# Gathers of the expert groups written in eight pieces and the sums to the tokens in two, between the phases of the chunks

## The chip, the cores and the metric

The kernel runs on one core of one Trainium2 chip. The metric is device time in microseconds, the median of several executions. The engines are TensorE (PE, its weight loads listed apart as PEld), VectorE (DVE), ScalarE (ACT), GpSimd (POOL) and SyncE (SP), which issues nearly all loads from HBM here.

## What is computed

A two-layer decoder trunk on 256 tokens and 16 meta tokens, width 1024. Layer 0 ends in a dense SwiGLU, layer 1 in a mixture of eight experts, of which each token takes two. The change touches only that mixture:

```python
def moe_swiglu(h, router_w, w_gate, w_up, w_down):
    logits = jnp.einsum('btd,de->bte', h, router_w).astype(jnp.float32)
    top_logits, top_idx = lax.top_k(logits, TOP_K)
    top_w = jax.nn.softmax(top_logits, axis=-1)
    combine = jnp.sum(jax.nn.one_hot(top_idx, N_EXPERTS, dtype=jnp.float32) * top_w[..., None], axis=-2)
    out = jnp.zeros_like(h)
    for e in range(N_EXPERTS):
        out = out + combine[..., e:e + 1] * swiglu(h, w_gate[e], w_up[e], w_down[e])
    return out
```

An expert's three matrices are 1024x3584, 1024x3584 and 3584x1024 in float32.

## The kernel before

Everything ahead of the experts (attention, short convolution, the gated recurrence, the dense layer, the router) is the same in both kernels.

**Experts and their order.** The router ranks the experts by their number of tokens. Rank 0 to 3 are Wide (L1085): up to 128 tokens, held as a high and a low half of 128 columns each. Rank 4 to 7 are Narrow (L1112): up to 64 tokens, high and low half side by side in 128 columns. Experts are put in groups that share one gathered matrix of tokens: group 0 is Wide 0 alone, groups 1 to 3 are a Narrow and then a Wide expert (4 and 1, 5 and 2, 6 and 3), group 4 is Narrow 7 alone. So the order is Wide 0, Narrow 4, Wide 1, Narrow 5, Wide 2, Narrow 6, Wide 3, Narrow 7 (L1189). `experts` (L1146) runs over them, and within an expert over seven chunks of 512 hidden columns (c = 0 to 6). A second call stands in a branch for experts with more tokens than fit (L1192) and is not taken with these inputs.

**A chunk.** `gate_up` (L1030) forms the gate products (tile psg), calls `between`, and forms the up products (psu). `between` (L1175) holds, once for a group, `weights` (the tokens' weights, tile wsp), and always `turn` of the chunk before: PE transposes the hidden values (hps), ACT and DVE split them. After `gate_up`, `finish` (L1160) forms the down products of the chunk before (tile y). A Wide chunk has 24 gate, 24 up and 24 down matmuls of 512 columns, a Narrow one 16 of each.

**Weights.** `MoveWeights` (L840) loads 1 MB at a time into one of seven buffers (six loads to a chunk), and each half is split in two: ACT copies the high part (h_g, h_u, h_d, L856) and DVE subtracts for the low part (l_g, l_u, l_d, L857). Seven pairs of such halves can be ahead.

**The gather.** `Group.__init__` (L994) multiplies the normed tokens (hnh, hnl) by a one-hot matrix (oh). For each of eight 128-row pieces k there are four matmuls (tile gat), one ACT copy and one DVE cast into x (L999 to L1006). It runs whole, ahead of chunk 3 of the last expert of the group before (L1171). The tile gat comes from `wtile` (L834), a pool of two PSUM banks that the weights' tile wsp, the turn of the one-hot matrix (cps) and the sums (sc) share.

**The sums.** When an expert's last down products are done, `combine` (L1068) goes over two halves of 512 columns: ACT and DVE make the weighted result (yh, yl; one buffer each), four matmuls spread it to the tokens (sc, L1079 and L1080), and two DVE adds (L1081) put it on the residual hst. As the down products run one chunk late, this stands after the up products of chunk 0 of the next expert.

**Order on the engines.** The source gives an order of priority. The build then puts each engine's instructions in a fixed order, in which an instruction whose inputs are ready can stand ahead of some that the source names first; each engine works through that order.

Of the kernel before, what the change touches and what calls it, by code (L numbers as in the profile page):

```python
# [19 lines left out]
P = 128  # L20
D = 1024
KD = D // P
# [29 lines left out]
def trunk(ctx: ExitStack, tc: tile.TileContext, x, meta, n1g, n2g, w_in, qng, kng, dlam,  # L52
# [937 lines left out]
    class Group:  # L990
# [3 lines left out]
        def __init__(self, wq_, nq_, oh):  # L994
            self.oh, self.w, self.n = oh, wq_, nq_
            self.x = mo.tile([P, KD, 3 * P], F32R, tag="x", bufs=2, name="x")
            h0, h1 = 0 if wq_ is not None else P, P if nq_ is None else P + 64
            l0, l1 = 2 * P if nq_ is None else P + 64, 3 * P if wq_ is not None else 2 * P
            for k in range(KD):  # L999
                ps = wtile("gat")  # L1000
                for src, o, a0, a1 in ((hnh, 0, h0, h1), (hnl, 256, l0, l1)):
                    for t in range(2):
                        PE.matmul(ps[:, o:o + a1 - a0], src[:, t, k * P:(k + 1) * P], oh[:, t, a0:a1],
                                  start=(t == 0), stop=(t == 1))
                A.activation(self.x[:, k, h0:h1], ps[:, 0:h1 - h0], AF.Copy)
                V.tensor_copy(self.x[:, k, l0:l1], ps[:, 256:256 + l1 - l0])  # L1006
# [13 lines left out]
    class Expert:  # L1020
# [47 lines left out]
        def combine(self, ct):  # L1068

            ws = self.g.ws[:, self.i, 0:1]  # L1070
            for n in range(2):
                ns = slice(n * 512, n * 512 + 512)
# [3 lines left out]
                V.scalar_tensor_tensor(yl, self.y[n], ws, yh.bitcast(F32), op0=ALU.mult, op1=ALU.subtract)  # L1076
                for t in range(2):
# [4 lines left out]
                    if self.last:  # L1082
                        nc.sync.dma_start(out[0, t * P:(t + 1) * P, ns], hst[:, t, ns])

# [61 lines left out]
    def experts(plan, first=None):  # L1146

        def group(pl):
            w = next((q for q, k in pl if k is Wide), None)
            n = next((q for q, k in pl if k is Narrow), None)  # L1150
            oh = oh0 if first and pl is plan[0] else one_hot(w, n, pos_s, sel_s)
            return Group(w, n, oh)

        flat = [(gi, q, k) for gi, pl in enumerate(plan) for q, k in pl]
        groups = {0: group(plan[0])}
        if first:
            new_phase("silu_and_others")
        prev = None

        def finish(x, c, ht):  # L1160
# [3 lines left out]
            if c == NCE - 1:  # L1164
                x.combine(ct)

        for n, (gi, q, kind) in enumerate(flat):
            x = kind(place[q], groups[gi])
            x.last = n == len(flat) - 1
            for c in range(NCE):  # L1170
                if c == 3 and n + 1 < len(flat) and flat[n + 1][0] != gi:  # L1171
                    groups[gi + 1] = group(plan[gi + 1])
                ht = []

                def between():  # L1175
                    if c == 0 and not hasattr(groups[gi], "ws"):
                        groups[gi].weights()
                    if prev is not None:
                        ht.append(prev[0].turn(prev[2]))
                if first and n == 0 and c == 1:  # L1180
                    residual(1)
                h = x.gate_up(c, between)
                if prev is not None:
                    finish(prev[0], prev[1], ht[0])
                prev = (x, c, h)
        finish(prev[0], prev[1], prev[0].turn(prev[2]))

    residual(0)
    experts([[(0, Wide)]] + [[(q + WIDE - 1, Narrow), (q, Wide)] for q in range(1, WIDE)] + [[(NE - 1, Narrow)]], True)  # L1189

    cnt = nc.values_load(cmaxi[0:1, 0:1], min_val=0, max_val=S + P // 2)
    with tc.If(cnt > P):  # L1192
        V.tensor_single_scalar(pos_s[:, :, 0:WIDE], pos_s[:, :, 0:WIDE], -float(P), op=ALU.add)
        V.tensor_single_scalar(pos_s[:, :, WIDE:], pos_s[:, :, WIDE:], -float(P // 2), op=ALU.add)
        experts([[(q, Wide)] for q in range(NE)])
# [30 lines left out]
```

## Time and profile before

| | us |
|---|---|
| median of three executions | 1830.02 |
| their range | 1829.35 to 1831.63 |
| the profiled execution | 1831.06 |
| its span, first to last instruction | 1829.3 |

In the profile each engine has its busy time; "idle before" is the time an engine stood still ahead of an instruction, with what ended it (the releaser). TensorE's granted clock is given as a share of 2.4 GHz, so 0.50 is 1.2 GHz. The stretches below are cut from the end of a chunk's last gate matmul to the end of the next chunk's last one, so a stretch holds one chunk's worth of up, down and gate products.

### The profile page before, as it was taken

Reading aid. Unit: us, or ns where it says so; the run is one execution under the profiler, and the core shown is the slowest. Engines: PE = TensorE matmul, PEld = TensorE weight load, DVE = VectorE, ACT = ScalarE, POOL = GpSimd, SP = SyncE. Lnnn points to the kernel's source line nnn. Section 1 sums busy time; section 2 is a strip of 40 time slices with the busy share of each in tenths; the row PEclk is TensorE's granted clock in tenths of the full one; section 3 lists DMA queues with packets and bytes.
Section 4 is the critical chain, followed back from the end, with each engine's and each line's share of the span. In section 5 each row is a group of like instructions: output and inputs, shape, how many; then the busy total and the mean of one; then the engine's idle time right before and its main releaser. Section 6 shows DMA issues by size and latency. Waiting matters only on the chain.

```text
span 1829.3 us, 27972 instructions
## 1 busy us (share of the span) xinstructions
PE 1763.9 (96%) x10613; PEld 1515.4 (83%) x10613; DVE 1468.0 (80%) x1934; ACT 1179.2 (64%) x1587; POOL 110.4 (6%) x137
## 2 busy tenths in 40 slices
PE   8999999999999999999999999999999999999997
PEld 7888999999999889998788767776677866787665
DVE  7667757877567577577889999989998899988997
ACT  4366444544443664446778887768877688877786
POOL 5201201100011003012000000000000000000000
PEclk9999999999999999998999999999999999999999
DMA  7333554555554236656989999999999899999996
GB/s 214 101 99 93 169 177 162 165 181 185 167 179 139 70 95 189 187 196 234 343 321 368 366 394 371 360 330 352 394 387 372 315 345 395 394 351 352 362 388 232
DMA packets 266123, 479.96 MB, mean 262 GB/s; under 512 B 7636, under 2 KB 115228, under 8 KB 265980
## 3 DMA queue, kind: packets, MB, share of 16 engines
q1 hardware_dynamic: 265472, 477.20, 73.8%
q8 instruction: 85, 1.39, 0.3%
q0 software_dynamic: 368, 0.86, 0.2%
q14 instruction: 58, 0.48, 0.1%
q10 hardware_dynamic: 140, 0.04, 0.0%
HBM read 477.01 MB, written 1.05 MB: 261 GB/s over the span
## 4 chain that ended last, share of the span: by engine, by line
PE 49%; DVE 11%; issue 3%; ACT 3%; POOL 0%; DVEq 0%; ACTq 0%; POOLq 0%
DVE l_g L857 5%; PE psu L1119 4%; PE psu L1118 3%; PE y L1091 3%; PE y L1090 3%; PE y L1092 3%; PE psu L1091 3%; PE psg L1091 3%; PE psu L1092 3%; PE psu L1090 3%; PE psg L1092 2%; PE psg L1090 2%; PE proj L230 2%; PE proj L229 2%; PE proj L228 2%
## 5 line engine op out<-in xcount | busy, mean ns | idle before, releaser
L230 PE MATMUL proj<-hgh,lo_in 128*128 128x272 f32 (+1 forms) x1024 | 297.2, 290 | 4.6 <-DVE lo_in L224 4.6
L228 PE MATMUL proj<-hgh,hi_in 128*128 128x272 f32 (+1 forms) x1024 | 297.8, 291 | 0.2 <-DVE z L357 0.2
L229 PE MATMUL proj<-hgl,hi_in 128*128 128x272 f32 (+1 forms) x1024 | 296.9, 290 | 0.0
L857 DVE TENSOR_TENSOR l_u<-r_u,h_u 128x1024 fp32r<-128x1024 f32 x224 | 265.3, 1220 | 28.2 <-ACT h_u L856 25.1
L857 DVE TENSOR_TENSOR l_d<-r_d,h_d 128x1024 fp32r<-128x1024 f32 x224 | 264.8, 1220 | 17.4 <-ACT h_d L856 15.4
L857 DVE TENSOR_TENSOR l_g<-r_g,h_g 128x1024 fp32r<-128x1024 f32 x224 | 265.4, 1220 | 5.8 <-ACT h_g L856 5.4
L223 ACT ACTIVATE hi_in<-raw_in 128x1024 fp32r<-128x1024 f32 x128 | 135.0, 1058 | 165.6 <-PE proj L229 150.3
L856 ACT ACTIVATE h_u<-r_u 128x1024 fp32r<-128x1024 f32 x224 | 227.4, 1053 | 15.6 <-PE y L1092 9.0
L856 ACT ACTIVATE h_g<-r_g 128x1024 fp32r<-128x1024 f32 x224 | 226.5, 1053 | 11.9 <-PE psu L1092 5.4
L856 ACT ACTIVATE h_d<-r_d 128x1024 fp32r<-128x1024 f32 x224 | 223.2, 1052 | 7.1 <-PE psg L1092 5.9
L230 PEld LDWEIGHTS proj<-hgh,lo_in 128*128 128x128 f32 x1024 | 193.9, 189 | 6.6 <-DVE lo_in L224 5.5
L228 PEld LDWEIGHTS proj<-hgh,hi_in 128*128 128x128 f32 x1024 | 194.1, 190 | 2.8 <-issue 1.1
L229 PEld LDWEIGHTS proj<-hgl,hi_in 128*128 128x128 f32 x1024 | 193.6, 189 | 2.4 <-issue 1.3
L224 DVE TENSOR_TENSOR lo_in<-raw_in,hi_in 128x1024 fp32r<-128x1024 f32 x128 | 158.5, 1240 | 33.6 <-ACT hi_in L223 33.3
L1119 PE MATMUL psg<-l_g,x 128*128 128x512 f32 x224 | 98.7, 441 | 20.3 <-DVE l_g L857 20.0
L1119 PE MATMUL psu<-l_u,x 128*128 128x512 f32 x224 | 98.2, 438 | 1.5 <-DVE l_u L857 1.5
L1119 PEld LDWEIGHTS psg<-l_g,x 128*128 128x128 f32 x224 | 41.9, 187 | 63.3 <-DVE l_g L857 57.6
L1091 PE MATMUL psg<-l_g,x 128*128 128x512 f32 x224 | 91.2, 407 | 3.1 <-DVE l_g L857 2.8
L1090 PE MATMUL psg<-h_g,x 128*128 128x512 f32 x224 | 90.3, 403 | 0.0
L1118 PE MATMUL psu<-h_u,x 128*128 128x512 f32 x224 | 90.1, 402 | 0.0
L1090 PE MATMUL psu<-h_u,x 128*128 128x512 f32 x224 | 89.9, 401 | 0.0
L1092 PE MATMUL psg<-h_g,x 128*128 128x512 f32 x224 | 89.8, 401 | 0.0
(404 smaller groups left out, 4124.5 us busy)
## 6 DMA issues: line engine op xcount, KB each, us to landing
r_g<-in_moe_w_gate_dram SPq DMA_DIRECT2D x112, 1024.0 KB, 7.0
r_u<-in_moe_w_up_dram SPq DMA_DIRECT2D x112, 1024.0 KB, 7.7
r_d<-in_moe_w_down_dram SPq DMA_DIRECT2D x110, 1024.0 KB, 7.9
raw_in<-in_w_in_dram SPq DMA_DIRECT2D x64, 1024.0 KB, 5.9
raw_br<-in_w_branch_dram SPq DMA_DIRECT2D x12, 1024.0 KB, 5.5
raw_fg<-in_ffn_w_gate_dram SPq DMA_DIRECT2D x11, 1024.0 KB, 5.3
raw_fu<-in_ffn_w_up_dram SPq DMA_DIRECT2D x11, 1024.0 KB
raw_wo<-in_w_out_dram SPq DMA_DIRECT2D x8, 1024.0 KB, 4.9
```

The costliest lines, as they stand in the source:

```text
L223: A.activation(hi, r, AF.Copy)
L224: V.tensor_tensor(lo, r, hi.bitcast(F32), op=ALU.subtract)
L228: PE.matmul(ps, sh, mh, start=first, stop=False)
L229: PE.matmul(ps, sh, ml, start=False, stop=False)
L230: PE.matmul(ps, sl, mh, start=False, stop=last)
L856: ih = raw_ins(A.activation(hi, r, AF.Copy))
L857: il = raw_ins(V.tensor_tensor(lo, r, hi.bitcast(F32), op=ALU.subtract))
L1090: PE.matmul(ps, st[0], hi, start=first, stop=False)
L1091: PE.matmul(ps, st[0], lo, start=False, stop=False)
L1092: PE.matmul(ps, st[1], hi, start=False, stop=last)
L1118: PE.matmul(ps, st[0], hi, start=first, stop=False)
L1119: PE.matmul(ps, st[0], lo, start=False, stop=last)
```

## The change

The experts keep their order. Three things move.

1. A group is made without its gather; `gather(k)` does one piece. Making the group and its one-hot matrix stands at the start of the chunk three ahead of the group's first one (two ahead for group 1). The eight pieces go on a list, `todo`.
2. `short` takes pieces off the list: two while more than four are left, else one, after the gate products (in `between`, ahead of `turn`) and after the up products, and one after the down products. What is left is done when the group begins. Group 0's gather is written whole at the start, as before.
3. `combine` makes the first half of the weighted result at once and returns two steps: the first puts half 0 to the tokens and makes half 1, the second puts half 1. They go to the head of the list; the first is taken right away by the `short()` behind `finish`, the second by the one after the next chunk's gate products.

The calls are turned from a plan of experts into a flat list of chunks, with the same chunks in the same order.

```diff
--- before.py
+++ after.py
@@ -996,14 +996,17 @@
             self.x = mo.tile([P, KD, 3 * P], F32R, tag="x", bufs=2, name="x")
             h0, h1 = 0 if wq_ is not None else P, P if nq_ is None else P + 64
             l0, l1 = 2 * P if nq_ is None else P + 64, 3 * P if wq_ is not None else 2 * P
-            for k in range(KD):
-                ps = wtile("gat")
-                for src, o, a0, a1 in ((hnh, 0, h0, h1), (hnl, 256, l0, l1)):
-                    for t in range(2):
-                        PE.matmul(ps[:, o:o + a1 - a0], src[:, t, k * P:(k + 1) * P], oh[:, t, a0:a1],
-                                  start=(t == 0), stop=(t == 1))
-                A.activation(self.x[:, k, h0:h1], ps[:, 0:h1 - h0], AF.Copy)
-                V.tensor_copy(self.x[:, k, l0:l1], ps[:, 256:256 + l1 - l0])
+            self.h, self.l = (h0, h1), (l0, l1)
+
+        def gather(self, k):
+            (h0, h1), (l0, l1) = self.h, self.l
+            ps = wtile("gat")
+            for src, o, a0, a1 in ((hnh, 0, h0, h1), (hnl, 256, l0, l1)):
+                for t in range(2):
+                    PE.matmul(ps[:, o:o + a1 - a0], src[:, t, k * P:(k + 1) * P], self.oh[:, t, a0:a1],
+                              start=(t == 0), stop=(t == 1))
+            A.activation(self.x[:, k, h0:h1], ps[:, 0:h1 - h0], AF.Copy)
+            V.tensor_copy(self.x[:, k, l0:l1], ps[:, 256:256 + l1 - l0])
 
         def weights(self):
 
@@ -1067,13 +1070,18 @@
 
         def combine(self, ct):
 
+
             ws = self.g.ws[:, self.i, 0:1]
-            for n in range(2):
-                ns = slice(n * 512, n * 512 + 512)
+
+            def prepare(n):
                 yh = mo.tile([P, 512], F32R, tag="yh", bufs=YB, name="yh")
                 yl = mo.tile([P, 512], F32R, tag="yl", bufs=YB, name="yl")
                 A.activation(yh, self.y[n], AF.Copy, scale=ws)
                 V.scalar_tensor_tensor(yl, self.y[n], ws, yh.bitcast(F32), op0=ALU.mult, op1=ALU.subtract)
+                return yh, yl
+
+            def put(n, yh, yl):
+                ns = slice(n * 512, n * 512 + 512)
                 for t in range(2):
                     ps = wtile("sc")
                     PE.matmul(ps, ct[:, t, :], yh, start=True, stop=False)
@@ -1081,6 +1089,15 @@
                     V.tensor_tensor(hst[:, t, ns], hst[:, t, ns], ps, op=ALU.add)
                     if self.last:
                         nc.sync.dma_start(out[0, t * P:(t + 1) * P, ns], hst[:, t, ns])
+
+            y0 = prepare(0)
+            y1 = []
+
+            def first():
+                put(0, *y0)
+                y1.extend(prepare(1))
+
+            return [first, lambda: put(1, *y1)]
 
     class Wide(Expert):
 
@@ -1143,56 +1160,79 @@
     place = [0] + [nc.values_load(ixi[0:1, q:q + 1], engines=[mybir.EngineType.SP], min_val=0, max_val=NE - 1)
                    for q in range(1, NE)]
 
-    def experts(plan, first=None):
-
-        def group(pl):
-            w = next((q for q, k in pl if k is Wide), None)
-            n = next((q for q, k in pl if k is Narrow), None)
-            oh = oh0 if first and pl is plan[0] else one_hot(w, n, pos_s, sel_s)
-            return Group(w, n, oh)
-
-        flat = [(gi, q, k) for gi, pl in enumerate(plan) for q, k in pl]
-        groups = {0: group(plan[0])}
-        if first:
-            new_phase("silu_and_others")
-        prev = None
+    def experts(groups, order, first=None):
+
+
+        made, xs = {}, {}
+        todo = []
+
+        def group(gi):
+            w, n = groups[gi]
+            made[gi] = Group(w, n, oh0 if first and gi == 0 else one_hot(w, n, pos_s, sel_s))
+
+        def short(n=1):
+            for _ in range(min(n, len(todo))):
+                todo.pop(0)()
 
         def finish(x, c, ht):
             if c == NCE - 1:
                 ct = x.combine_turn()
             x.down(c, ht)
             if c == NCE - 1:
-                x.combine(ct)
-
-        for n, (gi, q, kind) in enumerate(flat):
-            x = kind(place[q], groups[gi])
-            x.last = n == len(flat) - 1
-            for c in range(NCE):
-                if c == 3 and n + 1 < len(flat) and flat[n + 1][0] != gi:
-                    groups[gi + 1] = group(plan[gi + 1])
-                ht = []
-
-                def between():
-                    if c == 0 and not hasattr(groups[gi], "ws"):
-                        groups[gi].weights()
-                    if prev is not None:
-                        ht.append(prev[0].turn(prev[2]))
-                if first and n == 0 and c == 1:
-                    residual(1)
-                h = x.gate_up(c, between)
+                todo[0:0] = x.combine(ct)
+
+        starts = {}
+        for i, (gi, q, kind, c) in enumerate(order):
+            starts.setdefault(gi, i)
+        group(0)
+        for k in range(KD):
+            made[0].gather(k)
+        if first:
+            new_phase("silu_and_others")
+        prev = None
+        for i, (gi, q, kind, c) in enumerate(order):
+            for gj, at in starts.items():
+                if at == i + (2 if first and gj == 1 else 3):
+                    group(gj)
+                    todo.extend([lambda g=made[gj], k=k: g.gather(k) for k in range(KD)])
+                if at == i and i:
+                    short(len(todo))
+            if (gi, q) not in xs:
+                xs[gi, q] = kind(place[q], made[gi])
+                xs[gi, q].last = False
+            x = xs[gi, q]
+            x.last = i == len(order) - 1
+            ht = []
+
+            def between():
+                if not hasattr(made[gi], "ws"):
+                    made[gi].weights()
+                short(2 if len(todo) > 4 else 1)
                 if prev is not None:
-                    finish(prev[0], prev[1], ht[0])
-                prev = (x, c, h)
+                    ht.append(prev[0].turn(prev[2]))
+            if first and i == 1:
+                residual(1)
+            h = x.gate_up(c, between)
+            short(2 if len(todo) > 4 else 1)
+            if prev is not None:
+                finish(prev[0], prev[1], ht[0])
+                short()
+            prev = (x, c, h)
         finish(prev[0], prev[1], prev[0].turn(prev[2]))
+        short(len(todo))
 
     residual(0)
-    experts([[(0, Wide)]] + [[(q + WIDE - 1, Narrow), (q, Wide)] for q in range(1, WIDE)] + [[(NE - 1, Narrow)]], True)
+    order = []
+    for q in [0] + [p for i in range(1, WIDE) for p in (i + WIDE - 1, i)] + [NE - 1]:
+        k = Wide if q < WIDE else Narrow
+        order.extend((q if k is Wide else q - WIDE + 1, q, k, c) for c in range(NCE))
+    experts([(0, None)] + [(q, q + WIDE - 1) for q in range(1, WIDE)] + [(None, NE - 1)], order, True)
 
     cnt = nc.values_load(cmaxi[0:1, 0:1], min_val=0, max_val=S + P // 2)
     with tc.If(cnt > P):
         V.tensor_single_scalar(pos_s[:, :, 0:WIDE], pos_s[:, :, 0:WIDE], -float(P), op=ALU.add)
         V.tensor_single_scalar(pos_s[:, :, WIDE:], pos_s[:, :, WIDE:], -float(P // 2), op=ALU.add)
-        experts([[(q, Wide)] for q in range(NE)])
+        experts([(q, None) for q in range(NE)], [(q, q, Wide, c) for q in range(NE) for c in range(NCE)])
 
 
 # ---- launch: one core; inputs and outputs as the reference has them ----
```

## Rows read from the trace of the kernel before

**Rows 1.** The page, part 1: busy us, share of the span, instructions.

```profile
PE 1763.9 (96%) x10613; PEld 1515.4 (83%) x10613; DVE 1468.0 (80%) x1934; ACT 1179.2 (64%) x1587; POOL 110.4 (6%) x137
```

**Rows 2.** Busy by stretch: plain Wide, first, second, fourth group's gather, the next.

```profile
core 0: us, PE busy (x) PEld busy (x) DVE busy (x) ACT busy (x) POOL busy (x), PEclk, DMA share, GB/s
877.90:894.80 16.90, 16.90 (x78) 13.91 (x77) 15.63 (x15) 13.71 (x14) 0.00 (x0) 1.00 0.98 364
894.80:921.20 26.40, 24.26 (x110) 20.03 (x109) 18.31 (x23) 16.12 (x22) 0.00 (x0) 0.87 0.71 258
1132.79:1156.48 23.69, 21.38 (x107) 17.10 (x106) 21.17 (x26) 18.75 (x26) 0.00 (x0) 1.00 1.01 367
1617.00:1636.68 19.68, 19.68 (x103) 16.55 (x101) 16.07 (x20) 13.67 (x20) 0.00 (x0) 1.00 0.97 351
1636.68:1655.34 18.66, 18.36 (x87) 14.85 (x86) 15.39 (x16) 13.41 (x16) 0.00 (x0) 1.00 0.91 328
```

**Rows 3.** The same view: plain Narrow, three Wide-to-Narrow boundaries, one Narrow to Wide.

```profile
1261.26:1276.55 15.29, 14.52 (x66) 10.25 (x64) 14.47 (x15) 13.35 (x16) 0.00 (x0) 1.00 1.02 377
971.87:986.93 15.06, 15.06 (x71) 12.46 (x69) 14.25 (x14) 13.09 (x14) 0.00 (x0) 1.00 0.99 370
986.93:1002.63 15.70, 15.70 (x79) 13.03 (x78) 15.35 (x18) 13.93 (x18) 0.00 (x0) 1.00 1.03 390
1207.17:1225.57 18.40, 17.30 (x83) 13.52 (x81) 15.84 (x20) 13.52 (x16) 0.00 (x0) 1.00 0.92 323
1225.57:1245.64 20.07, 18.73 (x84) 13.54 (x82) 18.11 (x21) 16.22 (x21) 0.00 (x0) 1.00 0.88 316
1689.81:1705.90 16.09, 16.09 (x69) 11.86 (x68) 13.85 (x14) 12.65 (x14) 0.00 (x0) 1.00 1.00 371
1705.90:1725.98 20.08, 18.74 (x83) 13.52 (x82) 18.11 (x21) 16.22 (x21) 0.00 (x0) 1.00 0.93 347
1096.30:1116.56 20.26, 19.38 (x82) 14.04 (x81) 18.25 (x21) 15.93 (x18) 0.00 (x0) 1.00 1.03 383
```

**Rows 4.** Timeline of PE, first gather: start, us, instruction, [idle before, releaser].

```profile
906.04 0.36 PE L1003 MATMUL gat<-oh,hnh 128*128 128x192 f32 x2
...
906.91 0.41 PE L1090 MATMUL psg<-h_g,x 128*128 128x512 f32 x1
908.88 0.47 PE L1003 MATMUL gat<-oh,hnh 128*128 128x192 f32 x2 [1.56 <-DVE x L1006]
...
910.38 0.47 PE L1003 MATMUL gat<-oh,hnh 128*128 128x192 f32 x2 [0.37 <-DVE x L1006]
...
911.89 0.74 PE L1003 MATMUL gat<-oh,hnh 128*128 128x192 f32 x2 [0.21 <-DVE x L1006]
```

**Rows 5.** Busy time by stretch, within the first gather chunk.

```profile
911.20:918.00 6.80, 6.58 (x21) 5.41 (x21) 2.21 (x5) 2.29 (x5) 0.00 (x0) 0.50 0.12 41
```

**Rows 6.** Timeline of PE within up products, ahead of the second gather.

```profile
1136.05 0.25 PE L1003 MATMUL gat<-oh,hnl 128*128 128x192 f32 x1
...
1136.26 0.50 PE L1091 MATMUL psu<-l_u,x 128*128 128x512 f32 x1
1136.60 0.39 PE L1092 MATMUL psu<-h_u,x 128*128 128x512 f32 x1
```

**Rows 7.** Busy time by stretch of the gather's instructions alone (tile gat).

```profile
1132.79:1156.48 23.69, 4.64 (x29) 4.00 (x29) 2.63 (x8) 2.63 (x8) 1.00 1.01 367
1617.00:1636.68 19.68, 3.25 (x24) 3.61 (x24) 1.23 (x6) 1.34 (x6) 1.00 0.97 351
```

**Rows 8.** Waits, 1132 to 1157: us in total, times, longest.

```profile
ACT h L78 <- PE psg L1092: 6.1, 2, 5.8
ACT x L1005 <- PE gat L1003: 3.7, 3, 2.7
```

**Rows 9.** Lines L1076 and L1081 of the sums: ns min/median/max.

```profile
L1076 DVE SCALAR_TENSOR_TENSOR yl<-y,ws,yh x16: 742/746/750, 998.0 to 1821.0; 128x512 fp32r<-128x512 f32 x16
...
L1081 DVE TENSOR_TENSOR hst<-hst,sc x32: 677/680/687, 999.9 to 1822.9; 128x512 f32<-128x512 f32 x32
```

## The prediction

> **What bounds the kernel now.** I read the page first. TensorE is busy for 96% of the span [rows 1], but that is an average over a first half that the change leaves alone and a mixture of experts, the second half, that it rearranges. So I cut the mixture of experts into chunks: each stretch runs from the end of one chunk's last gate matmul to the end of the next one's. A chunk is one 512-column slice of an expert, seven per expert. Four kinds appear.
>
> A plain Wide chunk takes 16.90 us and PE is busy for all of it, DVE for 15.63 [rows 2]: PE bounds it. A plain Narrow chunk takes 15.29; PE is busy 14.52 and DVE 14.47 [rows 3], neither alone fills it, the two hand work to each other with about 0.8 us of waits. The third kind is the chunk that holds a gather: 26.40 us for the first of the four groups gathered here, 23.69 for the second, and the third's chunk is like the second's (two such chunks) [rows 2]. The fourth kind is the stretch after an expert ends, where its sums to the tokens stand: 20.07 from Wide to Narrow, 20.26 from Narrow to Wide [rows 3].
>
> In the gather chunks PE has holes: 26.40 against 24.26 busy, 23.69 against 21.38 [rows 2]. The PE rows show what they are: after each pair of pieces PE waits for the DVE cast of an earlier piece, 1.56, 0.37 and 0.21 us [rows 4], because a piece's PSUM tile comes from two buffers (wtile, L831) and is free only when both casts are done. In the first of these chunks the clock falls as well: it is granted at 0.50, the 1.2 GHz level, for the 6.80 us that begin after the first two of those waits [rows 5].
>
> **The change, part by part.** Instructions are neither added nor removed: 32 matmuls, 8 ACT copies and 8 DVE casts per group, and the same sums. They are moved.
>
> *Gather of a group in eight pieces.* The source wrote them as one lump ahead of chunk 3 of a Wide expert. Now it writes at most two pieces at a place: in the first of two chunks 2 after the gate products, 2 after the up products and 1 after the down products, in the second the last 3 one by one at the same three places. These are chunks 5 and 6 for the first group, 4 and 5 for the others. No DMA is issued by any of it, so SP's queue is passed by nothing. The weight loads wait for DVE's conversions to free their buffers. The DMA share is 0.88 to 1.03 in all stretches but the first gather's, at 316 to 390 GB/s [rows 2, 3]. A chunk is six loads of 1.05 MB; in 16.90 us that asks for 372 GB/s, under the 390 seen, so I charge nothing for loads. Without that reserve a chunk would gain nothing from a shorter gather.
>
> What stays is PE time, since these chunks are PE-bound. Eight gather matmuls took 906.04 to 906.91, so 0.109 us each [rows 4]; 32 make 3.5 us. Each interruption of a weight product costs a little: the up matmul at 1136.26 after a gather is followed at 1136.60, 0.34 later, where plain ones stand 0.23 apart (16.90 us hold 72 such matmuls and four transposes) [rows 2, 6]. That is 0.11 for each of six places, 0.7. Together 4.2 us for a group. The fourth group checks this: its gather is already strewn by the build over the products, and with 24 of its matmuls in it [rows 7] the chunk takes 19.68 with no PE hole [rows 2], 2.78 above plain, 0.116 for each.
>
> So the first group goes from 9.50 (26.40 less 16.90) to 4.2: 5.3 us gained, of which the half clock is 3.4 (half of 6.80). The second goes from 6.79, plus 0.3 for the three of its 32 matmuls that stand before the stretch (29 are in it [rows 7]), to 4.2: 2.9; the third likewise 2.9; the fourth is strewn now and gains nothing. Sum 11.1 us.
>
> What the pieces may cost: each one's copy stands in ACT's order and its cast in DVE's, in front of weight conversions, and both wait for PE to reach the piece. The bounds are 0 (the 19.68 chunk, no hole [rows 2]) and the hole after a piece in a lump, 1.56, 0.37 and 0.21, mean 0.71 [rows 4], for each of 32 pieces: 22.8 us. I take 0.3 a group, the hole of the chunk 18.66 against 18.36 that follows the strewn gather [rows 2], because that is the nearest to what the source will now write: 1.2 us. DVE has room for its part: 8 casts took 2.63 us [rows 7] and two Wide chunks leave it 2 times 1.27 [rows 2]. What is not covered there is taken from its lead.
>
> A rule that speaks against the change: the Trainium skill (TensorE: Matmul & The Clock Gate, section on the array as 16 sub-arrays) says that ScalarE and VectorE take their queues strictly in order while TensorE alone pulls weight loads ahead. The trace agrees: ACT sat 6.1 us in two waits for a gate product and 3.7 in three for a gather [rows 8] with conversions behind it. By that rule alone every piece would be one more such stop; that is the third rival below.
>
> *Sums in two parts.* Only the last four matmuls and two DVE adds of an expert move, behind the gate products of the next chunk. The DVE work at a boundary stays: two of 0.746 and four of 0.680, 4.2 us [rows 9]. From Wide to Narrow the chunk is 4.78 above plain, so at most 0.6 can go, in three places; from Narrow to Wide at most the PE hole, 20.26 less 19.38, 0.9, in three places [rows 3]: 4.5 in all. On the other side, the two adds (1.36) now stand ahead of DVE's part of the turn; uncovered, seven times, 9.5 us lost. What covers them is the time from the turn to the down products, one set of up products, some 3.6 to 5.5 us of PE. I take a gain of 1.0, near zero, since in both kinds the bounding work is unmoved. The last expert's tail runs both parts at once, as before.
>
> Sum: 11.1 plus 1.0 less 1.2 is 10.9 us. The profiled execution took 1831.06, its span 1829.3 with 1.8 around it; it becomes 1820.2. It stood 1.04 above the median 1830.02, so on the median's scale **1819.1**.
>
> **Rivals.** *The lump comes back, or the pieces were pieces already.* The order on an engine is not the source's: part of the second group's gather stands two at a time within up products of the chunk before [rows 6]. If the build gathers the pieces where it sees PE free, only the lost clock returns: 3.4, 1826.6; if it also falls, no change. Against: the lump was written as a lump and mostly remained one [rows 4].
>
> *The lead is lost at the first boundary.* From the first Wide expert to Narrow the first two stretches take 15.06 and 15.70, while the first and last of the three later such boundaries take 18.40 and 20.07, 16.09 and 20.08 [rows 3]. There conversions run ahead enough, here they don't. The first group's pieces now stand right before the cheap boundary; made like the second it costs 7.7 more: 1826.8. The opposite can happen too: the later three become like the first (7.7 and 5.4 at the ends, the middle between: some 20 us), 1799.
>
> *Casts hold the converters (slower).* The mechanism is the in-order stop above: ACT and DVE stand at a piece until PE reaches it, and then start the next weights too late for PE. The gathers now cost 9.5, 7.1, 7.1 and about 3.0, 26.7 in sum; afterwards three times 4.2, the same 3.0, and 32 times the hole for each piece. It decides from 0.35 us a piece; at the 0.71 of the lump the sum is 38.3, 11.6 slower: 1841.6. For it: ACT's waits [rows 8]. Against: the strewn gather with no hole [rows 2].
>
> The clock in the gather: it fell once, after the waits of 1.56 and 0.37, and stayed full in the second chunk with as much hole (2.31) [rows 2, 4, 5]. The Trainium skill (same page, section on a second failure mode) tells of PE idling briefly between groups as it cycles PSUM buffers and of the clock swinging for it; by it each lump would lose its clock, by the rows one did.
>
> **How the numbers follow.** Forecast (1815 to 1824): 0.52. Lump or pieces already: 0.13. Lead lost: 0.10. Converters held: 0.16. Lead gained: 0.09. A measurement of this kernel tells about 0.2% (3.7 us) from no change, so faster is under 1826.4 and slower above 1833.7. Faster takes the forecast, the lead gained, and half of the two that sit on the border: 0.71; same 0.12; slower 0.17. The range for 8 in 10 leaves out the lead gained and most of the held converters: 1809 to 1834.
>
> **What would show it.** Right: the chunks that hold pieces take 18 to 19.5 us with PE busy throughout, chunk 3 of the first expert is 16.9, the clock stays full after the first gather, and PE's waits for casts of x are gone except in the very first gather. Wrong: PE waits for l_g or l_u in the chunks with pieces (converters held); a first Wide-to-Narrow boundary of 18 to 20 us a stretch (lead lost); gather matmuls in runs of 12 and more (lump); or plain chunks that leave 16.90 and 15.29, which would mean that the build's order settled elsewhere, and which I have not priced.

## The result and the profile after

The kernel after takes 1818.73 us (median of six runs, 1817.16 to 1821.66); the kernel before, run beside it, 1831.84. The ratio is 0.9935, 95% interval [0.9925, 0.9946], so 11.9 us of 1831.84, between 9.9 and 13.7. The forecast was 1819.1. (Ratios here are the ones given with the runs; they lie nearer to the quotient of the means than to that of the medians.)

The two profiled spans are 1829.3 and 1817.2 us, 12.1 apart. The page of the kernel after, span and part 1:

```profile
span 1817.2 us, 27939 instructions
PE 1760.7 (97%) x10613; PEld 1510.5 (83%) x10613; DVE 1467.5 (81%) x1934; ACT 1176.9 (65%) x1587; POOL 110.5 (6%) x137
```

PE has as many instructions as before and is busy 3.2 us less; the rest of the gain was idle time. The 3.2 is a balance: 3.8 less in the stages of group 1's gather, where half a clock had cost 3.4 [rows 5], and 2.6 less up to there, against some 3 more in the later stages and the tail. Where the time went, from the same cuts as before (end of a chunk's last gate matmul to the end of the next one's), differences of the two traces added up stage by stage:

| stage | difference, us | forecast |
|---|---|---|
| first chunk of Wide 0, from its first gate product (14.50, now 11.68) | -2.8 | not foreseen |
| group 1's gather, Wide 0 chunk 3 to Narrow 4 chunk 0 | -5.9 | -5.3, +0.3 for holes |
| Narrow 4, the rest (first sums) | -0.6 | sums: -1.0 in all |
| Wide 1, with group 2's gather | -1.6 | -2.9, +0.3 |
| Narrow 5 | -0.2 | 0 |
| Wide 2, with group 3's gather | -1.6 | -2.9, +0.3 |
| Narrow 6, Wide 3 with group 4's gather, Narrow 7 | -0.5 | +0.3 |
| after the last gate products | +1.1 | 0 |

So the total came out as forecast, but only group 1's line did so for its own reason.

Busy time by stretch of the kernel after: columns as in [rows 2]. The first four are the last plain Wide chunk of Wide 0, the two that hold group 1's pieces, and the first Narrow chunk behind them; then Wide 1 (its chunks 2 to 6) and the boundary to Narrow 5.

```profile
925.82:942.71 16.89, 16.89 (x79) 13.96 (x77) 15.64 (x15) 13.70 (x14) 0.00 (x0) 1.00 1.01 371
942.71:961.83 19.12, 19.12 (x98) 16.17 (x98) 17.05 (x20) 14.90 (x19) 0.00 (x0) 1.00 0.98 344
961.83:978.22 16.39, 16.39 (x83) 13.78 (x82) 15.21 (x17) 13.99 (x18) 0.00 (x0) 1.00 0.97 350
978.22:993.79 15.57, 15.57 (x75) 12.65 (x75) 15.11 (x18) 14.59 (x19) 0.00 (x0) 1.00 1.03 385
1106.19:1123.36 17.17, 17.04 (x77) 13.88 (x77) 16.02 (x15) 10.51 (x11) 0.00 (x0) 1.00 1.02 380
1123.36:1142.01 18.65, 18.49 (x87) 15.16 (x86) 15.64 (x17) 13.80 (x17) 0.00 (x0) 1.00 1.00 364
1142.01:1160.14 18.13, 17.97 (x83) 14.61 (x83) 16.50 (x16) 12.99 (x15) 0.00 (x0) 1.00 0.99 344
1160.14:1177.92 17.78, 17.78 (x83) 14.47 (x83) 14.30 (x16) 12.94 (x16) 0.00 (x0) 1.00 0.96 356
1177.92:1196.26 18.34, 18.34 (x87) 14.66 (x85) 16.80 (x18) 13.21 (x16) 0.00 (x0) 1.00 0.97 349
1196.26:1214.66 18.40, 17.31 (x83) 13.52 (x81) 15.85 (x20) 13.53 (x16) 0.00 (x0) 1.00 0.93 330
1214.66:1233.55 18.89, 18.23 (x84) 13.57 (x82) 16.94 (x19) 14.60 (x18) 0.00 (x0) 1.00 0.95 336
```

Group 1's chunk of 26.40 [rows 2] is gone; its pieces add 2.23 to one chunk (19.12 less 16.89) and 1.33 to the next (16.39 less the 15.06 of [rows 3]), PE never stands still and the clock is full. In Wide 1 the chunk of 23.69 is gone as well, but four chunks are now 0.9 to 1.75 above the 16.90 that they or their like took.

PE's timeline shows how the groups differ. First a place of group 1, then two of group 2 (columns as in [rows 4]):

```profile
942.32 0.39 PE L1109 MATMUL psg<-h_g,x 128*128 128x512 f32 x1
942.54 0.36 PE L1006 MATMUL gat<-oh,hnh 128*128 128x192 f32 x2
942.74 0.39 PE L1006 MATMUL gat<-oh,hnl 128*128 128x192 f32 x2
...
943.41 0.60 PE L1121 MATMUL hps<-ident,h 128*128 128x128 f32 x4
...
1148.08 0.25 PE L1006 MATMUL gat<-oh,hnl 128*128 128x192 f32 x1
1148.17 0.41 PE L1108 MATMUL y<-l_d,hth 128*128 128x512 f32 x1
...
1153.95 0.36 PE L1006 MATMUL gat<-oh,hnh 128*128 128x192 f32 x2
1154.47 0.50 PE L1108 MATMUL psg<-l_g,x 128*128 128x512 f32 x1 [0.16 <-DVE l_g L857]
```

Group 1 stands as the source wrote it: two pieces behind the gate products, ahead of the turn, six places in all. Groups 2 and 3 are strewn by the build over 18 places, mostly single matmuls between two products, and some products behind them wait for a low part. The waits of these chunks (us in total, times, longest):

```profile
ACT x L1008 <- PE gat L1006: 11.2, 7, 3.1
ACT h L78 <- PE psg L1109: 9.4, 5, 5.8
...
PEld psu L1108 <- DVE l_u L857: 0.7, 3, 0.3
PEld y L1108 <- DVE l_d L857: 0.7, 3, 0.4
PEld psg L1108 <- DVE l_g L857: 0.7, 2, 0.3
...
PE psg L1108 <- DVE l_g L857: 0.3, 2, 0.2
```

This is 1106.19 to 1196.26, chunks 2 to 6 of Wide 1: ACT stands 11.2 us at pieces, and PE and its weight loads wait 2.4 us for low parts. In the two chunks of group 1 (942.71 to 978.22) the same view lists no wait of ACT for a piece and none of PE for a low part.

### The profile page after: what moved, and what is told of

It reads as the page before. It is cut to its first block, busy times and chain, and to the rows that moved or that the text cites. A ratio compares the mean times of both kernels' runs of the same rounds, so it can differ in the third digit from the quotient of the medians.

```text
span 1817.2 us, 27939 instructions
## 1 busy us (share of the span) xinstructions
PE 1760.7 (97%) x10613; PEld 1510.5 (83%) x10613; DVE 1467.5 (81%) x1934; ACT 1176.9 (65%) x1587; POOL 110.5 (6%) x137
## 4 chain that ended last, share of the span: by engine, by line
PE 48%; DVE 11%; issue 4%; ACT 3%; POOL 0%; DVEq 0%; ACTq 0%; POOLq 0%
DVE l_g L857 5%; PE psu L1136 3%; PE psg L1108 3%; PE psu L1108 3%; PE y L1107 3%; PE psu L1135 3%; PE y L1108 3%; PE psg L1109 3%; PE psu L1109 3%; PE psu L1107 3%; PE psg L1107 3%; PE y L1109 3%; PE proj L230 2%; PE proj L229 2%; PE proj L228 2%
## 5 line engine op out<-in xcount | busy, mean ns | idle before, releaser
L1136 PE MATMUL psu<-l_u,x 128*128 128x512 f32 x224 | 98.5, 440 | 0.3 <-DVE l_u L857 0.3
L1108 PE MATMUL psu<-l_u,x 128*128 128x512 f32 x224 | 90.1, 402 | 0.3
L1108 PE MATMUL y<-l_d,hth 128*128 128x512 f32 x224 | 90.3, 403 | 0.0
```

Of the source, the lines that this page charges most:

```text
L1108: PE.matmul(ps, st[0], lo, start=False, stop=False)
L1136: PE.matmul(ps, st[0], lo, start=False, stop=last)
```

## The experiments

What was open: which of the two parts, and which of the three mechanisms in group 1 (holes, clock, place), carries the gain; why groups 2 and 3 gave half of what was expected; whether pieces in Wide chunks hold the converters or spend a lead that the next boundary needs.

**Each part alone.** The pieces without the sums in two (first diff), and the sums in two with the old lump ahead of chunk 3 (second):

```diff
-            return [first, lambda: put(1, *y1)]
+            first()
+            put(1, *y1)
+            return []
```
```diff
-                if at == i + (2 if first and gj == 1 else 3):
+                if at == i + 4:
...
-                    todo.extend([lambda g=made[gj], k=k: g.gather(k) for k in range(KD)])
+                    for k in range(KD):
+                        made[gj].gather(k)
```

> The gather in pieces as in the changed kernel, the sums to the tokens whole as before. If the gain is the gather's (my theory), it is 11 to 13 us faster than before, 1818 to 1821, and the first chunks after a boundary are those of before (20.1 and 15.6 from Wide to Narrow, 20.3 and 16.2 from Narrow to Wide). If the sums in two parts carry 3 us or more of it, it stays at 1822 or above.

> The gather as one lump ahead of chunk 3 as before, the sums in two parts. By my theory the later half only moves a microsecond from one chunk to the next: 1829 to 1832, no change, with boundary chunks of about 18.9 and 16.6 (Wide to Narrow) and 19.3 and 17.2 (Narrow to Wide). If the split sums gain by themselves: 1825 to 1828.

Measured: pieces alone 1818.39 against 1830.20, ratio 0.9941 [0.9927, 0.9954], the whole gain; sums alone 1828.35, 0.9999 [0.9989, 1.0009], nothing. The boundary Wide 1 to Narrow 5, its second stretch and the one after, with the sums whole (first two rows) and in two (the last two, from the run with sums alone):

```profile
1214.68:1234.72 20.04, 18.69 (x83) 13.52 (x82) 18.11 (x21) 16.20 (x21) 0.00 (x0) 1.00 0.88 317
1234.72:1250.42 15.70, 14.32 (x65) 10.41 (x64) 14.83 (x15) 12.02 (x15) 0.00 (x0) 1.00 1.00 368
```
```profile
1223.19:1242.11 18.92, 18.25 (x84) 13.61 (x82) 16.96 (x19) 14.61 (x18) 0.00 (x0) 1.00 0.92 334
1242.11:1258.66 16.55, 15.14 (x66) 10.17 (x64) 15.93 (x17) 13.62 (x17) 0.00 (x0) 1.00 0.93 331
```

35.74 against 35.47: the second half of the sums moves about a microsecond of PE and DVE work into the next stretch and saves 0.3. The time of sums alone cannot tell that from nothing, since its interval is 1.8 us wide to either side.

**Place or pieces.** All eight pieces written together, but at the new place:

```diff
-                    todo.extend([lambda g=made[gj], k=k: g.gather(k) for k in range(KD)])
+                    for k in range(KD):
+                        made[gj].gather(k)
```

> The changed kernel, but a group's eight pieces are written at one place, where the changed kernel begins with them (chunk 5 of the first expert, chunk 4 of the others). If the cutting in pieces counts, PE's waits for the casts of x come back: about 2 us of holes in each of three gather chunks, 1826 to 1832, the upper end if the clock falls again. If the later place counts and not the pieces: 1818 to 1820, as the changed kernel.

Measured 1826.04 against 1830.20, 0.9981 [0.9972, 0.999]. Stretches: group 1's lump, the part of it at half clock, group 2's lump.

```profile
925.95:951.75 25.80, 24.25 (x111) 20.36 (x109) 18.31 (x23) 16.12 (x22) 0.00 (x0) 0.87 0.71 251
940.60:947.40 6.80, 6.80 (x27) 6.00 (x26) 2.15 (x6) 1.99 (x6) 0.00 (x0) 0.50 0.42 149
1146.85:1168.43 21.58, 20.09 (x98) 16.03 (x97) 19.72 (x23) 16.55 (x22) 0.00 (x0) 1.00 1.00 357
```

With the lump the hole (1.55 us ahead of the third piece) and the half clock are back in group 1, at another place. Being in pieces is what counts for most of the gain. The late lump is still 3.5 us under the kernel before (1.8 to 5.1 by the interval); group 2's lump, 21.58 here and 23.69 [rows 2] before, is one part of it, so the place is not worth nothing.

**Fewer places.** The pieces begin a chunk earlier for groups 2 to 4 and two earlier for group 1, ahead of chunk 3:

```diff
-                if at == i + (2 if first and gj == 1 else 3):
+                if at == i + 4:
```

> The changed kernel, but the pieces begin at chunk 3, where the lump was. If the pieces count and the place doesn't: 1817 to 1821, no difference to the changed kernel. If pieces must stand late: 1823 or more.

Measured 1815.68 against 1830.20, 0.9925 [0.9911, 0.994], under both forecasts; by medians 3 us under the kernel after, by the ratios 1.8, with overlapping intervals. Group 2's pieces stand at 12 places instead of 18, and its six chunks take 108.05 instead of 109.34. The last of the three chunks with group 2's pieces (18.29 and 18.20 the two ahead of it), then the boundary's first stretch:

```profile
1159.16:1177.38 18.22, 18.22 (x90) 15.23 (x90) 16.52 (x18) 15.20 (x19) 0.00 (x0) 1.00 1.00 356
...
1194.28:1212.68 18.40, 17.30 (x83) 13.52 (x81) 15.84 (x20) 13.60 (x16) 0.00 (x0) 1.00 0.94 330
```

The boundary stays at 18.40, though a plain chunk of 16.90 now lies between the last piece and it; distance alone did not win the lead back.

**Pinned.** Each gather matmul ordered behind the last weight product that the source wrote ahead of it, so the build cannot strew it:

```diff
...
+                    if last_pe:
+                        tc.add_manual_dep(i, last_pe[0].name, nosync, reason="place")
...
-            PE.matmul(ps, st[1], hi, start=False, stop=last)
+            last_pe[:] = [raw_ins(PE.matmul(ps, st[1], hi, start=False, stop=last))]
...
```

> The changed kernel, with each gather matmul ordered behind the last weight product that the source writes ahead of it, so that the build can't draw it forward into the products. In the changed kernel the second and third group's matmuls stand in some 18 places and cost about 5.5 us a group, the first group's in five places 3.6. If the strewing is what halves the gain there, the two groups now cost 3.6 each and the time falls by 3 to 5 us against the changed kernel (14 to 17 us under before). If the strewn ones fill time that PE would lose anyway, it is as the changed kernel or slower.

> The pieces begin at chunk 3 and each is held to its place. Alone, the early place gave about 3 us and the held place about 4 against the changed kernel. If these are separate (the early place spares the boundary, the held place the strewing), 1810 to 1813; if both work by the lead at the boundary, no better than one alone, 1814 to 1816.

Measured 1814.27 against 1830.27, 0.9909 [0.9892, 0.9925]. Chunk 4 of Wide 1, ahead of the pieces, with no gather matmul in it; then its last chunk and the boundary:

```profile
1144.23:1161.47 17.24, 17.24 (x79) 13.75 (x78) 14.99 (x15) 12.66 (x14) 0.00 (x0) 1.00 0.99 364
...
1180.18:1198.40 18.22, 18.22 (x91) 15.23 (x90) 17.38 (x19) 15.83 (x19) 0.00 (x0) 1.00 1.00 353
1198.40:1213.47 15.07, 15.07 (x72) 12.46 (x69) 11.93 (x12) 10.39 (x11) 0.00 (x0) 1.00 1.04 392
1213.47:1233.42 19.95, 19.28 (x98) 14.97 (x96) 17.76 (x24) 14.53 (x19) 0.00 (x0) 1.00 0.84 297
```

Six places now, as forecast for the change itself. The Wide chunks give 0.8 us (108.50 for the six), and the boundary 2.3: 15.07 and 19.95, 35.02, where it was 18.40 and 18.89, 37.29. The time is in the forecast range, but holding the pieces to their places gave only the 0.8 a group; the boundaries gave more. Both together (pinned, and begun early; the two diffs joined): 1811.86 against 1829.68, 0.9902 [0.9885, 0.9918], boundary 15.59 and 20.65. That time lies with "separate", the trace does not: from the first gate product to the end the joined run takes 960.0 us, pinned alone 959.1 and the kernel after 965.6. What the joined run's profile is shorter by came ahead of the experts, so by the traces it is no better than pinned alone.

**The gather's matmuls twice.** Each gather product of groups 1 to 4 done a second time into the same sum's place, the result unchanged; 128 extra matmuls.

```diff
...
-                for t in range(2):
+                for t in (0, 1, 0, 1) if twice[0] else (0, 1):
...
```

> The changed kernel, with the gather matmuls of groups 1 to 4 done twice over (128 more; the second set writes the same sums). If a piece costs its PE time since the Wide chunks are PE-bound, 128 times 0.109 us or 14 us more than the changed kernel, 2 us slower than before. If PE has room there, under 7 us more.

Measured 1816.95 against 1830.27, 0.9928 [0.9911, 0.9945]: not slower than the kernel after at all. The last chunk of Wide 1, and the boundary:

```profile
1181.98:1201.55 19.57, 19.57 (x103) 16.57 (x102) 18.08 (x20) 15.17 (x18) 0.00 (x0) 1.00 1.04 379
1201.55:1216.60 15.05, 15.05 (x71) 12.45 (x69) 14.25 (x14) 13.07 (x14) 0.00 (x0) 1.00 1.01 356
1216.60:1232.02 15.42, 15.42 (x76) 12.65 (x75) 15.02 (x20) 13.05 (x17) 0.00 (x0) 1.00 1.02 384
```

The work is paid for where it stands: Wide 1 takes 112.06 instead of 109.34. At the boundary it comes back more than whole: 30.47 instead of 37.29. While PE does extra work in a Wide chunk, ACT and DVE go on converting. Worked out from the trace (end of a low part to the start of the first product that reads it, mean over the gate products of the first Narrow chunk), conversions were 0.07 us ahead of PE there in the kernel after and 5.07 us here. What PE waited for at this boundary in the kernel after (1196.26 to 1233.55), and with doubled matmuls no longer waits for at all:

```profile
PE psg L1136 <- DVE l_g L857: 1.5, 2, 1.1
...
PEld psg L1136 <- DVE l_g L857: 3.6, 5, 1.5
```

So PE waits for DVE's low parts there, and five microseconds of lead pay for the sums. In group 1 the extra matmuls are not repaid (some 2.4 us stay); the lead there was 5.9 us already.

**Pieces in Narrow chunks.** Groups 2 to 4 one piece a chunk, from the third chunk of the Narrow expert before, so that few are left for the Wide one (8 of group 2's 32 matmuls in chunks 1 to 6 of Wide 1):

```diff
-                if at == i + (2 if first and gj == 1 else 3):
+                if at == i + ((2 if gj == 1 else 12) if first else 3):
...
-                short(2 if len(todo) > 4 else 1)
+                short(1 if i > 7 else 2)
...
```

> The changed kernel, with the pieces of groups 2 to 4 one to a chunk from chunk 2 of the Narrow expert on, where PE stands idle 0.77 us and DVE 0.8 us of a 15.29 us chunk. If that idle time is free for a piece (0.44 us of PE, 0.3 of ACT and DVE), five pieces of each group cost nothing: 6 to 9 us under the changed kernel. If the chunk is a chain from DVE to PE that every added cast lengthens by its own 0.36 us or more, it is as the changed kernel within 2 us or slower.

Measured 1812.33 against 1830.27, 0.9903 [0.9887, 0.992], by medians 6.4 under the kernel after. The last chunk of Wide 1, with no gather matmul in it, and the boundary:

```profile
1177.59:1194.84 17.25, 17.23 (x77) 13.75 (x77) 14.99 (x15) 12.67 (x14) 0.00 (x0) 1.00 1.00 361
1194.84:1210.92 16.08, 16.07 (x70) 11.87 (x68) 13.84 (x14) 12.67 (x14) 0.00 (x0) 1.00 1.00 361
1210.92:1229.83 18.91, 18.24 (x83) 13.68 (x83) 16.96 (x19) 14.62 (x18) 0.00 (x0) 1.00 0.99 366
```

In Narrow 4 the pieces cost 0.85 us in all (this run was 0.47 us earlier than the kernel after ahead of them and 0.38 later behind them); in Narrow 5 two chunks take 17.08 and 16.31 where 16.58 and 15.29 stood. The boundary, rid of the pieces just ahead of it, falls to 34.99. So the time met the forecast, but the pieces are not free in Narrow chunks; the gain stands in the Wide experts (the six chunks of Wide 1 107.57 instead of 109.34, of Wide 3 106.38 instead of 109.28) and at the boundaries.

**ACT's stops taken away.** ACT's two steps on the hidden values (h and hth), which wait for PE with conversions queued behind them, ordered behind the chunk's last up conversion. Then the same with the pieces in Narrow chunks:

```diff
...
-            act(h, psg, AF.Silu, scale=self.g.ws[:, 0, 1:2])
+            tc.add_manual_dep(act(h, psg, AF.Silu, scale=self.g.ws[:, 0, 1:2]), self.up.name, nosync, reason="lead")
...
-            A.activation(hth, ps3, AF.Copy)
+            held[:] = [raw_ins(A.activation(hth, ps3, AF.Copy))]
...
```

> The changed kernel, with ACT's two copies that wait for PE in a Wide chunk (h, which waits for the gate products, and hth, which waits for the turn) ordered behind that chunk's last conversion of up weights. The low parts are ready 6 us ahead of their matmul in the first expert and under 1 us in the later Wide ones, and the boundaries after these take 34 to 37 us for two stretches, after the first expert 32. If the lead is lost because ACT stands in order at those two copies, leads of 2 us or more come back in the later Wide experts and the three boundaries fall by 3 to 7 us each: 6 to 17 us under the changed kernel, 1802 to 1813. If ACT and DVE lack the time to get ahead, the leads stay under 1.5 us and the time is as the changed kernel or, for the later turn, slower.

> Both: the pieces of groups 2 to 4 within Narrow chunks, as in the run that did this alone and took 1812, and the two ACT copies behind the up conversions. If the two gains are of different places, 1797 to 1808; if both come from the same boundaries, as the better of the two alone.

Measured 1814.45 against 1829.68, 0.9921 [0.9905, 0.9938]; joined, **1806.53**, 0.9872 [0.9855, 0.9888], which is 23 us under the kernel before and some 12 under the one after. One chunk of Wide 1 and the boundary in the first; the last chunk of Wide 1 and the boundary in the second:

```profile
1140.93:1158.57 17.64, 17.64 (x83) 14.54 (x83) 16.22 (x16) 12.38 (x15) 0.00 (x0) 1.00 0.98 353
1194.31:1212.24 17.93, 17.18 (x83) 13.55 (x81) 14.49 (x19) 11.03 (x13) 0.00 (x0) 1.00 0.93 343
1212.24:1232.05 19.81, 18.73 (x84) 13.36 (x82) 17.70 (x20) 15.09 (x19) 0.00 (x0) 1.00 0.88 322
```
```profile
1176.83:1193.74 16.91, 16.91 (x77) 13.92 (x77) 14.89 (x15) 13.01 (x14) 0.00 (x0) 1.00 1.01 377
1193.74:1208.93 15.19, 15.19 (x69) 12.17 (x68) 13.19 (x13) 10.40 (x11) 0.00 (x0) 1.00 1.00 371
1208.93:1228.68 19.75, 18.59 (x83) 13.42 (x83) 17.43 (x20) 15.09 (x19) 0.00 (x0) 1.00 0.97 359
```

The first of these did not do what was expected of it: the boundary stayed at 37.74. Its gain is in the Wide chunks instead (107.52 for the six of Wide 1, was 109.34). With the pieces out of the way as well the boundary takes 34.94, as it did with the pieces in Narrow chunks alone (34.99). What ACT's order adds there is again in the Wide chunks: without a gather matmul the last chunk of Wide 1 takes 16.91, where it took 17.25 without that order. The two gains are of different places and add up (by medians 4.3 and 6.4, joined 12.2), as the first of the two forecasts had it.

**The kernel before once more**, for one look at the clock at the start of the experts:

> The kernel before once more, for its clock: in the first profile the clock was at half from 846.4 us on for 17.1 us, in five profiles since for 6.8 us. If that length changes by itself, this span is 1826 to 1827 with 6.8 us at half; if it belongs to this kernel, 1829 with 17 us again.

Measured: a span of 1831.0. The stretch at half clock, in both profiles of the kernel before and in that of the kernel after:

```profile
846.40:863.40 17.00, 15.66 (x62) 13.90 (x63) 12.77 (x52) 7.37 (x16) 2.12 (x7) 0.50 0.20 64
```
```profile
847.80:864.80 17.00, 15.86 (x62) 14.05 (x62) 12.45 (x51) 7.53 (x16) 2.12 (x7) 0.50 0.18 64
```
```profile
849.00:855.80 6.80, 6.80 (x28) 6.02 (x27) 6.59 (x31) 3.78 (x8) 0.75 (x4) 0.50 0.44 157
```

## Why the prediction was right, and where it was not

**Group 1: right, for the reason given.** The step said 9.50 becomes 4.2. It became 3.56 (2.23 and 1.33), gain 5.9. Pieces at six places, no hole, full clock; the late lump shows that hole and clock return with the lump.

**The own price of a gather: nearly right, one term wrong.** 32 matmuls at 0.109 were confirmed, the 0.7 for interruptions were not. From the timeline I added up, over chunks 1 to 6 of Wide 1, the time from each gather matmul to the start of the next instruction, and what the starts of successive products stand apart beyond 0.226 us:

| Wide 1, us | before | after | pinned | ACT's stops gone |
|---|---|---|---|---|
| places of the gather | 7 | 18 | 6 | 18 |
| gather, with products' waits ahead of it | 7.0 | 4.3 | 3.4 | 3.5 |
| spacing of products beyond 0.226 | 2.9 | 4.2 | 4.2 | 3.2 |
| six chunks | 110.87 | 109.34 | 108.50 | 107.52 |

At 18 places a gather costs 3.5 if nothing waits, as much as at 6. Interrupting the products had no price of its own.

**Groups 2 and 3: the mis-sized term.** The gain was to be 2.9 less 0.3 for each; it was 1.5. In the kernel after, 0.8 us stand at the gather beyond its 3.5, and 1.3 us more than before lie between products: 2.1 us a group, where 0.7 and 0.3 had been put. I read the 0.3 off idle time, and PE's idle time is indeed only 0.45 a group (holes of 0.13, 0.16 and 0.16 in the rows above). But most of the loss is not in the idle column: it shows on PE as products a little further apart, all of it busy.

The third rival, the held converters, would lay this on the stops at the pieces, 0.26 us a piece beyond the 3.5 (0.17 beyond the 4.2 on which its deciding 0.35 was reckoned). What the runs leave to them is the 0.8 at the gather. The 1.3 comes without them as well: with the pieces pinned it all stands in chunks 2 to 4 of Wide 1, which hold no gather matmul, and the two chunks that hold the 32 add 0.03; with pieces in Narrow chunks 1.1 of it stands in chunks 4 to 6, which hold none.

What failed is the 16.90 under the sum. Behind a lump, whose holes give ACT and DVE time, the gate and up conversions of a Wide chunk are 5.7 to 6.4 us ahead (chunk 4 of Wide 1 in the kernel before) and it takes 16.90; with 0.5 to 1.4 us it takes 17.24 even where no gather stands in it (17.24 pinned, 17.25 with pieces in Narrow chunks, rows above). Such a chunk stood in the kernel before too, in Wide 3, where the gather is strewn and no lump gives a pause:

```profile
1655.34:1672.58 17.24, 17.24 (x78) 13.75 (x77) 15.46 (x15) 12.66 (x14) 0.00 (x0) 1.00 0.98 359
```

Its six chunks took 109.46 there; Wide 1 and 2 now take 109.34 and 109.31. The prediction's check on the fourth group read one chunk of it (19.68) and of the next, 18.66 without a gather matmul, the 0.3 of hole alone. Two of its signs of being wrong came: PE waits for l_g in chunks with pieces (0.3 us above), and plain chunks leave 16.90, which it had not priced.

Taking ACT's stops at h and hth away gave back 1.8 us a group, 0.3 of it in a chunk without pieces, though ACT's stops at the pieces grew (the same view there):

```profile
ACT x L1010 <- PE gat L1008: 18.0, 8, 3.9
```

With the pieces out of the way too, the plain chunk is back at 16.91 (row above). So the loss does come from converters that stand still in their order, but mainly at the hidden values, in chunks without lead, and not at the pieces. The Trainium skill's sentence on strict order in ACT and DVE (TensorE: Matmul & The Clock Gate, section on the array as 16 sub-arrays), which the prediction set against the change, thus has its effect here, at a far smaller price than the stops are long: 11.2 us of stops at pieces and 9.4 at h stand beside 2.1 us of PE.

What tells the groups apart is the lead of the conversions, worked out as above: 5.7 to 7 us in the Wide chunks ahead of group 1's pieces, 0.2 to 1.7 in those of groups 2 and 3. With the matmuls done twice the lead in the last two chunks of Wide 1 grows to 2.6 to 7, and 64 of them cost 0.12 each.

**Group 4: right.** It was strewn before and after; its four chunks took 74.99 before and 74.78 after.

**The lead at the boundaries.** Neither side of that rival came: the first boundary takes 16.39 and 15.57, which is 15.06 and 15.70 with 1.33 of gather in it, and the later ones are still dear (18.40, then 18.89). But the gain of that rival exists: pinned pieces, pieces in Narrow chunks and doubled matmuls each bring the first stretch of the later boundary from 18.40 to 15.05 to 16.08. The prediction took it for something that the change would either hit or miss; with doubled matmuls it is a quantity that PE's own work in the Wide chunks fills. Distance alone (pieces begun early) does not, and neither does taking ACT's stops away alone. The leads over the gate products of Narrow 5's first chunk, worked out as above, explain only part of it: 0.07 in the kernel after and 0.08 with pieces begun early (both 18.40), 3.33 pinned and 5.07 doubled (15.07 and 15.05), but 0.07 too with pieces in Narrow chunks (16.08). Why that one falls is open; I have no rule that would have told it beforehand.

**Sums in two.** Forecast -1.0; alone 0.9999, which cannot tell 1.0 from nothing. In the traces, the kernel after against pieces alone, they give 0.2 to 0.3 in each of Narrow 5, 6 and 7, 0.7 in all. The -0.6 in Narrow 4 is not theirs: pieces alone have it (92.57 for its chunks 1 to 6, where the kernel before has 93.15), sums alone do not (93.09). It belongs to the pieces of group 1, by a way that stays open.

**Two errors that cancelled.** The profile's first Wide chunk gave 2.8 us that no step held, because the clock was at half for 17.0 us before and for 6.8 after, over the same instructions; the tail took 1.1 back (26.46 to 27.59, with half clock from 1808.2 in the kernel after). Without both, the steps as they ran give 12.1 less 1.7, 10.4, beside 10.9 forecast. That these lie so near is luck as well: groups 2 and 3 gave 2.0 less than forecast, group 1 0.9 and the remaining stages 0.6 more.

The 2.8 seem to belong to single executions. Both profiles of the kernel before show 17.0, but sums alone, with the same instructions up to that point, had the shorter stretch (11.92 for that chunk). And of the 23 runs of the kernel before beside the first four experiments, six have a mean granted clock of 0.996 or 0.997 and took 1825.58 to 1827.70; the other seventeen have 0.992 to 0.994, as its two profiles do, and took 1828.40 to 1832.54. The 10.2 us between the two stretches, at half clock, are 0.003 of that mean. No trace of such a run was kept. If it is so, some 3 to 4 of the 11.9 us are not the change's: the six have their median 7.6 above the kernel after.

## What to carry to other kernels

Breaking a lump of dependent small matmuls into pieces between long products removed the holes of its PSUM ring, and with them the clock drop that stood in the first lump; where the pieces landed mattered less here than that they were pieces. What a stage then costs is read from the lead of the producers there, not from PE's idle column: with 6 us of lead the pieces cost their own PE time; with 1 us or so products stand a little further apart, in chunks with pieces and in chunks without. A plain chunk's time is therefore a base only for chunks with the same lead, and a lump's pause can be what keeps the chunks behind it short. And PE work put into a PE-bound stage that is followed by one that waits for its producers isn't always lost: here it came back as lead at the boundary, so price a step by both stages.

## What the runs showed of the hardware that was not expected

The granted clock at the start of the experts fell to 0.50 in every profile, for 17.0 us in both profiles of the kernel before, for 10.2 with pieces pinned and begun early, for 6.8 in the kernel after and the others; in the kernel after PE's instructions stand in the same order as before up to 906 us there. Later it fell in each lump of group 1 (three kernels: 911.2 in the kernel before [rows 5], 906.5 with sums alone, 940.6 with the late lump), always after holes of 1.55 us or so, and once in a lump of group 2 (3.4 us from 1148.9 with sums alone); it fell in no gather of groups 1 to 4 that was in pieces, in nine kernels. The prediction's reading that one lump loses its clock and not each holds: group 2's lump of [rows 2], with 2.31 us of holes, kept it.

A matmul of the gather put singly between two products took 0.108 us at 18 places (ACT's stops gone) and at 6 (pinned) alike: where no operand was late, leaving and taking up a stream of 512-column products had no price of its own that could be read.
